# Loading an attention layer's constants through GpSimd's DMA queue instead of SyncE's

## The chip, the core and the metric

The kernel runs on one core of a Trainium2 chip. Such a core has five engines that each work through their own list of instructions in order: TensorE (PE in the profile; its weight loads are listed apart as PEld), VectorE (DVE), ScalarE (ACT), GpSimd (POOL) and SyncE (SP), which here does nothing but issue DMA transfers. Engines wait for one another through semaphores. The metric is the device time of one execution in microseconds (us), as a median over runs; lower is better.

## What is computed

One transformer layer on 256 tokens of width 2048, all in float32: an input projection, three attentions that share it (a forgetting attention with 6 heads, a sparse attention with 4 heads over compressed, selected and windowed keys, and an indexed top-k attention with 6 heads), a gated mixture of the three, and a gated feed-forward layer, each followed by a layer norm; a last gated addition ends it.

```
z = split_cols(h @ w_in[i])
o_fox = fox_attention(q, k, v, z['fox_f'], fox_f_bias[i])
o_nsa = nsa_attention(...)                    # rope, compression with nsa_pe_*, nsa_cmp_*
k_d, v_d = split(rms_norm(z['dsa_ckv'], dsa_kv_norm[i]) @ dsa_kv_up[i], 2)
o_dsa = dsa_attention(apply_rope(...), rope1(k_d, cos, sin), v_d, ...)
mixed = g_fox*(o_fox @ w_br_fox) + g_nsa*(o_nsa @ w_br_nsa) + g_dsa*(o_dsa @ w_br_dsa)
h = layer_norm(ALPHA * h + mixed @ w_out, ln1_g, ln1_b)
a, b = split(h @ w_ffn_in, 2)
h = layer_norm(ALPHA * h + (silu(a) * b) @ w_ffn_out, ln2_g, ln2_b)
h = h + (p @ w_ple_in) * sigmoid(h @ w_ple_gate)
```

Beside the weights the attentions need small constants: an identity matrix, cosine and sine tables for the rotary embedding ("rope"), a triangle of ones, masks, the vectors `dsa_kv_norm` and `fox_f_bias`, and the small matrices `kvup`, `peT` and `cmp2`.

## The kernel before

**Products.** Every float32 factor is split into a rounded part and a remainder (`halves`, line 156): ACT writes the rounded part (`whi`, `k4h`), DVE subtracts it from the source and writes the remainder (`wlo`, `k4l`). A product is then three matmuls: rounded by rounded, rounded by remainder, remainder by rounded (lines 246, 247, 248). The weights of the input projection come in chunks named c1, c2, c3, c4, c6, c5, c7 and f0 to f5. A chunk of 512 columns is loaded in eight groups of 512 KB (`raw<-att_c`, line 170; three `raw` buffers, so that a load waits until DVE has split the group three before it), and each group feeds 12 matmuls of 512 columns. Below, g1 to g8 are the groups of c2, the second chunk, and g9, g10 and so on those of c3.

**Work beside the chunks.** The attentions' own steps are generators that a counter of groups (`tick`) moves on, a few instructions after each group. `after_c1` takes the results of c1: it ropes the index keys (lines 544 to 548), takes a power of the mean square on GpSimd (`rms`, line 632), scales with `gkv` (line 639), transposes on TensorE (line 647), multiplies by `kvup` (line 658), ropes the product into `rc` and transposes it (line 555). A further generator, `prepare`, loads pieces of a later weight (`preb`, `prea`, line 902) and forms differences of them on DVE (lines 904 to 908).

**The constants.** `load` brings in one constant. It first lets GpSimd copy a single element of the newest remainder `wlo` into the destination's corner (line 513), which holds the transfer back until DVE has come that far, and then issues the DMA (line 514). `load_first` loads the first part of the table `cst`, `gkv` and `fbias` and copies the identity out of `cst` on DVE (line 520); `load_rest` loads `kvup`, the second and third part of `cst`, `peT` and `cmp2`. These are eight transfers in all. GpSimd issues no other transfer before the layer norm's parameters (`gb`, line 1090), far behind the attention.

**What sets the order.** The program is written as one stream; when it is built, a scheduler places each engine's instructions by its own estimate of when they can run. An edit of one engine's work can so move instructions on others, and from then on the order on each engine is fixed.

Of the kernel before, what the change touches and what calls it, by code (L numbers as in the profile page):

```python
# [128 lines left out]
def build(ctx: ExitStack, tc: tile.TileContext, A: dict):  # L129
    nc = tc.nc  # L130
# [150 lines left out]
    def pair_gemm(a, b, X, F, seven, kt, pool, banks, mid=None, out=None, slots=None, defer=False, long=0, spare=(),  # L281
# [70 lines left out]

        for p in range(np_ - long):
            ra, rb, raw, x = load(p)
            if p not in seven:
                w = ahead if p == 0 and ahead else [split(ra, "", wp), split(rb, "", wp)]
# [44 lines left out]
        if long:  # L401
            W = []
            for i, p in enumerate(range(np_ - long, np_)):
                ra, rb, _, x = load(p)
                name, q = spare[i - 2] if i >= 2 else ("", wp)
                W.append((p, x, [split(ra, name, q), split(rb, name, q)]))
            for h in range(2):
                for p, x, w in W:
                    plain(p, h, x, w)
                    tick()  # L410
                finals([h])
                if h == 0:
                    between()
            return e
# [48 lines left out]
    with ExitStack() as at:  # L463
# [43 lines left out]
        def load(tile, src, part=None):  # L507

            t = tile if part is None else tile[:, part]
            corner = t  # L510
            while len(corner.shape) > 2:
                corner = corner[:, 0]
            POOL.tensor_copy(corner[:1, :1], newest[0].bitcast(F32)[:1, :1])
            nc.sync.dma_start(t, src if part is None else src[:, part])

        def load_first():
            load(cst, A["consts"], slice(0, n1))
            load(gkv, A["dsa_kv_norm"].partition_broadcast(P))
            load(fbias, A["fox_f_bias"].partition_broadcast(P))
            DVE.tensor_copy(ident, C["ident"])  # L520
            POOL.memset(half_c, -0.5)
# [452 lines left out]
    part = ctx.enter_context(ExitStack())  # L974
# [416 lines left out]
```

## Time and profile before

| What | Value |
| --- | --- |
| Time, median of 3 runs | 1556.35 us (1555.92 to 1556.39) |
| The profiled execution's own time | 1554.99 us |
| Its span, first to last instruction | 1553.2 us |
| TensorE busy | 1544.1 us (99%) |
| DVE busy | 1363.2 us (88%) |
| ACT busy | 879.6 us (57%) |
| POOL busy | 20.8 us (1%), 44 instructions |
| Granted TensorE clock | 1.000 |

Times inside the span are counted from its start. A row of the timeline gives start, duration, engine, line, operation, `out<-in`, how many such instructions, and in brackets how long the engine sat idle before and what ended that. SP's rows (SPq) are the issues of transfers; when a transfer has landed is in the view of DMA issues, as microseconds from issue to landing. In the rows of `order` below, an instruction is given with its line, operation, tiles and shape and no time.

### The profile page before, as it was taken

How to read it: one execution, taken by the hardware profiler on the slowest of the kernel's cores; microseconds unless marked ns; L12 is line 12 of the kernel's file. 1: busy time of each engine (PE TensorE's matmuls, PEld its weight loads, DVE VectorE, ACT ScalarE, POOL GpSimd, SP SyncE). 2: the span in 40 equal slices, each digit the busy share in tenths (PEclk: the TensorE clock that was granted, in tenths of full speed). 3: DMA queues.
4: the chain of work that ended last, by engine and by line, in shares of the span. 5: the costliest groups of instructions: out<-in, count | busy, mean ns of one | idle time of the engine just before them, and what ended most of it. 6: DMA issues, size and time to landing. Idle time of an engine off the chain costs nothing. (4 is left out here: it accounts for less than half of the span.)

```text
span 1553.2 us, 20506 instructions
## 1 busy us (share of the span) xinstructions
PE 1544.1 (99%) x7317; PEld 1288.6 (83%) x7317; DVE 1363.2 (88%) x1909; ACT 879.6 (57%) x1153; POOL 20.8 (1%) x44
## 2 busy tenths in 40 slices
PE   9999999999999999999999999999999999999998
PEld 7778899988888888888788888888888888887887
DVE  6779787569898998998879999999999999989896
ACT  6545566556565555544455656665556666555463
POOL 1000000000000000001000000000000000010000
PEclk9999999999999999999999999999999999999999
DMA  8866888575655574648465667777777776887544
GB/s 293 295 216 215 303 287 290 175 218 207 217 176 186 208 255 155 225 164 298 152 223 188 230 234 246 263 257 264 274 261 268 259 265 227 293 284 250 175 165 135
DMA packets 105575, 360.91 MB, mean 232 GB/s; under 512 B 12033, under 2 KB 13185, under 8 KB 105473
## 3 DMA queue, kind: packets, MB, share of 16 engines
q1 hardware_dynamic: 104192, 355.41, 67.1%
q0 software_dynamic: 1280, 4.20, 0.9%
q8 instruction: 57, 0.93, 0.2%
q14 instruction: 46, 0.37, 0.1%
HBM read 337.54 MB, written 22.02 MB: 231 GB/s over the span
## 5 line engine op out<-in xcount | busy, mean ns | idle before, releaser
L156 ACT ACTIVATE whi<-raw 128x1024 fp32r<-128x1024 f32 (+3 forms) x538 | 507.2, 962 | 338.9 <-PE acc L247 96.3
L156 DVE TENSOR_TENSOR wlo<-raw,whi 128x1024 fp32r<-128x1024 f32 (+3 forms) x538 | 585.5, 1104 | 126.3 <-ACT whi L156 123.5
L246 PE MATMUL acc<-whi,k4h 128*128 128x512 f32 (+3 forms) x724 | 274.9, 380 | 0.5 <-ACT k4h L156 0.3
L247 PE MATMUL acc<-whi,k4l 128*128 128x512 f32 (+3 forms) x724 | 266.9, 369 | 0.8 <-DVE k4l L156 0.8
L248 PE MATMUL acc<-wlo,k4h 128*128 128x512 f32 (+3 forms) x724 | 266.3, 369 | 0.4 <-DVE wlo L156 0.4
L156 ACT ACTIVATE wthi<-raw 128x1024 fp32r<-128x1024 f32 x166 | 175.7, 1060 | 152.8 <-DVE raw L382 92.0
L156 DVE TENSOR_TENSOR wtlo<-raw,wthi 128x1024 fp32r<-128x1024 f32 x166 | 200.0, 1218 | 0.1
L299 PE MATMUL sc<-whi,k4h 128*128 128x512 f32 x488 | 191.2, 392 | 0.0
L300 PE MATMUL sc<-whi,k4l 128*128 128x512 f32 x488 | 190.1, 390 | 0.0
L301 PE MATMUL sc<-wlo,k4h 128*128 128x512 f32 x488 | 189.7, 390 | 0.1
L299 PE MATMUL acc<-whi,k4h 128*128 128x512 f32 x408 | 160.1, 392 | 0.0
L301 PE MATMUL acc<-wlo,k4h 128*128 128x512 f32 x408 | 159.1, 390 | 0.6 <-DVE wlo L156 0.6
L300 PE MATMUL acc<-whi,k4l 128*128 128x512 f32 x408 | 158.9, 389 | 0.0
L246 PEld LDWEIGHTS acc<-whi,k4h 128*128 128x128 f32 x724 | 136.3, 188 | 24.3 <-issue 5.1
L247 PEld LDWEIGHTS acc<-whi,k4l 128*128 128x128 f32 x724 | 136.5, 189 | 18.9 <-DVE k4l L156 1.5
L248 PEld LDWEIGHTS acc<-wlo,k4h 128*128 128x128 f32 x724 | 136.0, 188 | 19.5 <-DVE wlo L156 0.8
L382 DVE TENSOR_TENSOR raw<-raw 128x1024 f32<-128x1024 f32 x78 | 95.1, 1219 | 18.0 <-DMA raw<-ffn_in 6.2
L301 PEld LDWEIGHTS sc<-wlo,k4h 128*128 128x128 f32 x488 | 91.6, 188 | 19.8 <-DVE wlo L156 0.5
L300 PEld LDWEIGHTS sc<-whi,k4l 128*128 128x128 f32 x488 | 91.7, 188 | 18.9
L299 PEld LDWEIGHTS sc<-whi,k4h 128*128 128x128 f32 x488 | 91.6, 188 | 18.7
L301 PEld LDWEIGHTS acc<-wlo,k4h 128*128 128x128 f32 x408 | 76.5, 188 | 17.5 <-DVE wlo L156 1.5
L299 PEld LDWEIGHTS acc<-whi,k4h 128*128 128x128 f32 x408 | 76.7, 188 | 15.4
(381 smaller groups left out, 2115.3 us busy)
## 6 DMA issues: line engine op xcount, KB each, us to landing
raw<-ffn_in SPq DMA_DIRECT2D x169, 512.0 KB, 4.5
raw<-gate SPq DMA_DIRECT2D x96, 512.0 KB, 4.5
raw<-ffn_out SPq DMA_DIRECT2D x88, 512.0 KB, 4.9
raw<-att_c SPq DMA_DIRECT2D x40, 512.0 KB, 4.6
raw<-att_f SPq DMA_DIRECT2D x48, 384.0 KB, 3.9
raw<-ple_gate SPq DMA_DIRECT2D x32, 512.0 KB, 4.4
g<-actd SPq DMA_DIRECT2D x20, 512.0 KB, 4.7
g<-cmp SPq DMA_DIRECT2D x16, 512.0 KB, 5.5
```

Source lines behind the costliest of these rows:

```text
L156: split_last[:] = [ACT.activation(hi, src, AF.Copy).ins, DVE.tensor_sub(lo, src, hi.bitcast(F32)).ins]
L246: PE.matmul(o, xh[:, c], h, start=(k == 0), stop=False)
L247: PE.matmul(o, xl[:, c], h, start=False, stop=False)
L248: PE.matmul(o, xh[:, c], l, start=False, stop=(k == kt - 1))
L299: PE.matmul(o, xh, h, start=first, stop=False)
L300: PE.matmul(o, xl, h, start=False, stop=False)
L301: PE.matmul(o, xh, l, start=False, stop=stop)
L382: DVE.tensor_tensor(t[0], raw[:, 0:1, :].broadcast_to([P, 2, 512]), raw[:, 1:3, :], op=ALU.subtract)
```

## The change

The DMA of `load` is issued by GpSimd instead of SyncE. The same eight transfers, with the same copies in front of them, so leave SP's list and enter GpSimd's.

```diff
             POOL.tensor_copy(corner[:1, :1], newest[0].bitcast(F32)[:1, :1])
-            nc.sync.dma_start(t, src if part is None else src[:, part])
+            nc.gpsimd.dma_start(t, src if part is None else src[:, part])
```

The scheduler then builds three places differently. First the two queues themselves. On GpSimd, around the loads of `load_first` and the start of `load_rest`:

```order
 L513 COPY gkv<-wlo 1x1
 L513 COPY fbias<-wlo 1x1
+L514 DMA cst<-consts 128x448
+L514 DMA gkv<-dsa_kv_norm 128x256
+L514 DMA fbias<-fox_f_bias 128x6
 L513 COPY kvup<-wlo 1x1
+L514 DMA kvup<-kvup 128x512
+L513 COPY cst<-wlo 1x1
+L514 DMA cst<-consts 128x384
 L638 COPY ra<-ra 128x64
-L513 COPY cst<-wlo 1x1
```

The first transfer stands behind three copies, and the copy of `after_c1` (line 638) now stands behind five transfers. On SyncE, from the start of c2's loads:

```order
+L170 DMA raw<-att_c 128x1024 x3
+L902 DMA preb<-ffn_in 128x1024
+L170 DMA raw<-att_c 128x1024 x3
+L902 DMA prea<-ffn_in 128x1024
 L170 DMA raw<-att_c 128x1024
-L514 DMA cst<-consts 128x448
-L514 DMA gkv<-dsa_kv_norm 128x256
-L514 DMA fbias<-fox_f_bias 128x6
```

The loads of g1 to g6 follow one another with only `preb` between them, and `prea` is issued behind g6; before it was issued behind g7.

Second, on DVE, in the middle of c2, where `after_c1` scales its result (line 639):

```order
 L673 SCALAR_TENSOR_TENSOR lf<-lf 128x12
 L904 TENSOR_TENSOR pret<-preb 128x512
+L905 TENSOR_TENSOR pret<-preb,prea 128x512
 L639 SCALAR_TENSOR_TENSOR ra<-acc,rms,gkv 128x256 x2
 L156 TENSOR_TENSOR wlo<-raw,whi 128x1024 x2
```

The instruction that needs `prea` now stands in front of line 639 and of the splits of g5 and g6. On TensorE at the same place:

```order
-L248 MATMUL acc<-wlo,k4h 128x512
 L647 MATMUL sc<-ident,ra 128x128 x4
+L246 MATMUL acc<-whi,k4h 128x512
+L247 MATMUL acc<-whi,k4l 128x512
+L248 MATMUL acc<-wlo,k4h 128x512
```

The first four transposes of what line 639 writes stand six matmuls earlier, directly behind g3's matmuls.

Third, on DVE near the end of c2, in front of the first rope of `rc`:

```order
 L908 TENSOR_TENSOR prea<-prea,preb 128x512
+L156 TENSOR_TENSOR wlo<-raw,whi 128x1024
 L156 TENSOR_TENSOR pret<-pret,prea 128x512
-L156 TENSOR_TENSOR wlo<-raw,whi 128x1024
+L156 TENSOR_TENSOR wlo<-raw,whi 128x1024 x2
 L544 TENSOR_TENSOR rc<-sc,cst 128x128
```

Before, DVE had split eight groups of c2 and c3 ahead of this rope; now ten, so the rope stands behind the splits of g9 and g10.

## The prediction

> **What bounds the kernel now.** I began with the page's busy times and the table by stretches around the change.
>
> ```profile
> PE 1544.1 (99%) x7317; PEld 1288.6 (83%) x7317; DVE 1363.2 (88%) x1909; ACT 879.6 (57%) x1153; POOL 20.8 (1%) x44
> ...
> 0.00:10.00 10.00, 8.21 (x32) 6.62 (x32) 3.17 (x6) 5.15 (x8) 0.34 (x6) 1.00 0.77 251
> ...
> 20.00:30.00 10.00, 10.00 (x47) 8.57 (x46) 6.01 (x13) 5.97 (x14) 2.23 (x5) 1.00 0.75 262
> 30.00:40.00 10.00, 10.00 (x48) 8.30 (x47) 8.22 (x19) 6.39 (x11) 3.07 (x4) 1.00 0.96 337
> 40.00:50.00 10.00, 9.99 (x46) 7.93 (x45) 7.40 (x17) 4.92 (x8) 1.22 (x4) 1.00 0.77 273
> 50.00:60.00 10.00, 9.90 (x50) 8.38 (x51) 9.94 (x21) 5.39 (x9) 0.08 (x1) 1.00 0.91 295
> ```
>
> Columns after the length are the busy time of PE, PEld, DVE, ACT and POOL, then clock, DMA share and GB/s. TensorE sets the time: 9.1 us of the 1553.2 us span are not covered by it, 1.8 of them in the first 10 us, and in the 40 us where the constants are loaded only 0.11. So time can hardly be won here, while any microsecond for which TensorE waits goes into the end: it works in order and has no free time later to make it up.
>
> Next I looked at what SyncE waits for between 18 and 60 us, since that is what the edit takes away.
>
> ```profile
> SPq L514 <- POOL cst L513: 7.1, 2, 4.2
> ...
> SPq L514 <- POOL cmp L513: 5.2, 1, 5.2
> SPq L514 <- POOL gkv L513: 3.4, 1, 3.4
> ...
> SPq L514 <- POOL kvup L513: 1.7, 1, 1.7
> ```
>
> SyncE stands still for 7.1 + 5.2 + 3.4 + 1.7 = 17.4 us behind GpSimd's copies, with weight loads queued behind it. Freeing it lets those loads start earlier, but TensorE has no wait there that they could shorten.
>
> **The change part by part.** *Removed:* the 17.4 us of SyncE's waits, worth at most the 0.11 us above; I take 0. *Kept:* the eight copies and the bytes. *Added:* eight issues on GpSimd. That engine is idle, so the issues cost nothing by themselves; what counts is when the data land and who waits.
>
> *Step 1, the first constants land later.* The instruction that waits is DVE's copy of the identity (line 520), with DVE's split of g1 right behind it.
>
> ```profile
> 21.94 0.58 POOL L513 COPY cst<-wlo 1x1 f32<-1x1 f32 x1 [21.07 <-DVE wlo L156]
> 22.47 0.17 POOL L513 COPY gkv<-wlo 1x1 f32<-1x1 f32 x1
> 22.59 1.17 POOL L513 COPY fbias<-wlo 1x1 f32<-1x1 f32 x1
> ...
> 22.55 0.33 SPq L514 DMA_DIRECT2D cst<-consts  x1
> ...
> cst<-consts SPq DMA_DIRECT2D x1, 224.0 KB, 2.6
> ...
> 25.26 0.23 DVE L520 COPY ident<-cst 128x128 f32<-128x128 f32 x1 [0.94 <-DMA cst<-consts]
> 25.40 1.22 DVE L156 TENSOR_TENSOR wlo<-raw,whi 128x1024 fp32r<-128x1024 f32 x1
> ...
> 29.41 0.39 PE L248 MATMUL acc<-wlo,k4h 128*128 128x512 f32 x1
> ```
>
> Now SyncE issues as soon as the first copy is done, at 22.55, and the table lands 2.6 us later. In the changed list GpSimd issues only behind its third copy, at 22.59 + 1.17 = 23.8. The trace has no constants on GpSimd's queue; the nearest rows are the layer norm's parameters, the first of the bursts at 704, 1362, 1368 and 1378 us:
>
> ```profile
> gb<-ln_g POOLq DMA_DIRECT2D x1, 256.0 KB, 3.8
> ...
> gb<-ln_g POOLq DMA_DIRECT2D x1, 256.0 KB, 6.3
> ...
> gb<-ln_g POOLq DMA_DIRECT2D x1, 256.0 KB, 6.7
> ...
> gb<-ln_g POOLq DMA_DIRECT2D x1, 256.0 KB, 5.8
> ...
> L1090 POOL DMA_DIRECT2D gb<-ln_g x8 | 4.5, 564 | 610.0 <-PE sc L301 605.2 <-PE acc L301 4.8
> ```
>
> 3.8 to 6.7 us from issue to landing bound it: 27.6 to 30.5. I take 5.0, a little above the middle of the lowest two (3.8 and 5.8), since 224 KB is less than 256 but two loads of 512 KB (g3, `preb`) are issued beside it: landing at 28.8. The copy then ends near 28.9 and g1's split, 25.40 less 25.26 behind it and 1.22 long, at 30.3. TensorE needs it at 29.41: it waits **0.9**. At 27.6 the wait is 0; at 30.5 it is 2.6.
>
> The Trainium skill, "DMA: Bandwidth & Descriptors", section "Anatomy of one DMA — SWDGE (gpsimd) path", fits 2.0 us plus bytes over 436 GB/s for a transfer of this queue. That would be some 2.5 us for 224 KB, an estimate from that page; the table would land at 26.3 and this step would cost nothing. The 3.8 to 6.7 us just quoted speak against it in this kernel.
>
> *Step 2, the wait moves to `prea`.* DVE goes on with g2, the first rope and g3; then SyncE may issue g6 and behind it `prea`.
>
> ```profile
> 28.10 0.23 DVE L544 TENSOR_TENSOR ra<-zs,cst 128x64 f32<-128x64 f32 x1 [1.48 <-ACT zs L627]
> ...
> 28.63 0.18 DVE L548 TENSOR_TENSOR ra<-ra,rb 128x32 f32<-128x32 f32 x1
> ...
> 34.62 0.42 SPq L902 DMA_DIRECT2D prea<-ffn_in  x1
> ...
> preb<-ffn_in SPq DMA_DIRECT2D x1, 512.0 KB, 5.0
> ...
> prea<-ffn_in SPq DMA_DIRECT2D x1, 512.0 KB, 6.7
> ...
> 35.00 0.69 DVE L904 TENSOR_TENSOR pret<-preb 128x512 f32<-128x512 f32 x1
> 35.60 0.87 DVE L639 SCALAR_TENSOR_TENSOR ra<-acc,rms,gkv 128x256 f32<-128x256 f32 x2
> ...
> 37.11 0.39 PE L246 MATMUL acc<-whi,k4h 128*128 128x512 f32 x1
> ```
>
> 30.3 + 1.2 (g2) + 0.7 (rope) + 1.2 (g3) = 33.4; with SyncE's 0.4 for g6, `prea` is issued at 33.8, a little before today's 34.62. It landed 6.7 us after its issue, `preb` 5.0; today three loads stand ahead of `prea` within 3 us, in the change two. I take 5.0: 38.8. Line 905 now waits for that, and line 639, which today starts at 35.60, waits behind it: 38.8 + 0.7 (line 905, as line 904) + 0.4 (half of 0.87) = 39.9. The first transposes on TensorE stand where its matmul at 37.11 stood. TensorE is then **2.8 us** behind (the 0.9 of step 1 included, not added). With 27.6 and a landing in 4.6 it would be 1.2; with 30.5 and 6.7, 6.2.
>
> The table lands 3.6 us later than today's 25.2, yet only 2.8 comes through, since DVE's idle gap of 1.48 in front of line 544 takes up the rest.
>
> *Step 3, the rope of `rc` behind g10.*
>
> ```profile
> L156 DVE TENSOR_TENSOR wlo<-raw,whi 128x1024 fp32r<-128x1024 f32 x9 | 10.9, 1214 | 2.7 <-ACT whi L156 2.6
> ...
> 41.47 0.29 DVE L650 COPY nsT<-sc 128x128 f32<-128x128 f32 x1 [1.77 <-ACT nT L649]
> 41.68 0.28 DVE L651 COPY dkT<-sc 128x128 f32<-128x128 f32 x1
> ...
> raw<-att_c SPq DMA_DIRECT2D x1, 512.0 KB, 4.6
> ...
> raw<-att_c SPq DMA_DIRECT2D x1, 512.0 KB, 6.3
> ...
> 49.14 0.28 DVE L544 TENSOR_TENSOR rc<-sc,cst 128x128 f32<-128x128 f32 x1
> ...
> 49.73 0.22 DVE L548 TENSOR_TENSOR rc<-rc,rb 128x64 f32<-128x64 f32 x1
> ...
> 49.94 1.06 ACT L156 ACTIVATE whi<-raw 128x1024 fp32r<-128x1024 f32 x1 [0.67 <-DMA raw<-att_c]
> 50.10 0.30 PE L555 MATMUL sc<-ident,rc 128*128 128x128 f32 x1
> ```
>
> Today the rope ends at 49.95 and TensorE's transpose follows at 50.10 with 0.15 to spare. In the change g10's split stands ahead. Its load needs g7's buffer: 38.8 + 0.7 + 0.9 (line 639) + 3 x 1.2 (g5, g6, g7) + 0.6 (copies) = 44.6. It lands in 4.6 to 6.3 us (g6's row and g10's own); the middle gives 50.0. Then 1.06 on ACT, 1.2 on DVE, 0.8 for the rope: 53.1. TensorE would be **3.0** behind, nearly what step 2 left it with. With 4.6 the step adds nothing to step 2; with 6.3 it makes 3.9.
>
> *Other waits.* `gkv`, `kvup`, the tables' second part and `peT` are needed much later than they land, or in DVE's shadow of steps 1 and 2: cost 0. If `fbias` landed after DVE reached line 669 it would lengthen step 2 by up to 1; that is in the upper bound.
>
> *Sum.* Steps 2 and 3 overlap, so the larger nearly rules: 2.9. On the profiled execution's 1554.99 (span 1553.2 plus 1.8 around it): 1557.9. The median of the runs shown lies 1.36 higher, so the forecast is **1559.3**, 0.19% up. About 0.2%, 3.1 us, is what a measurement of this kernel can tell from no change; the forecast lies just under that line.
>
> **The rivals.** *The cover holds.* GpSimd's first transfer lands as fast as its fastest row or faster, `prea` comes while DVE still works, and TensorE loses 0 to 1.2: 1556.4 to 1557.6, say 1556.9. For it: DVE has idle gaps of 0.9 to 1.8 us there, and SyncE's weight loads come earlier. Against: three of the four first-of-burst rows are at 5.8 or above. (By the Trainium skill's fit, cited in step 1, this case would come about.)
>
> *Late landing, slower beyond doubt.* The first table lands 6.7 us after issue, at 30.5, and pushes every later split: from 29.1 on, step 2 exceeds 3.1 us. With `prea` in 5.0 this makes 30.5 - 28.8 = 1.7 more: 4.5, or 1560.9; with 6.7 too, 1562.6. For it: the transfer shares the DMA engines with two loads of 512 KB, at a DMA share of 0.75 to 0.96. Against: 3.8 in the first burst.
>
> The Trainium skill, "SBUF — State Buffer", section "SBUF: two separate sides", warns that GpSimd cannot write its descriptors while DVE runs a copy in a two-port mode, and tells of some 620 ns that became 3100. As an estimate from that page that is 2.5 us more on the first landing, about 1561.8. The 0.56 us per `gb` issue show no such stretch here, and DVE is idle from 24.3 on (the 0.94 in front of line 520), soon after the first issue.
>
> *SyncE's freedom pays.* Earlier weight loads take away waits beyond 60 us and outweigh steps 1 to 3: at most the 9.1 us not covered by TensorE less the 1.8 in the first 10 us, ahead of the change, or 7.3; with half of that, 1552.7.
>
> *It does nothing.* The two queues could behave alike: 1556.35. The list of GpSimd speaks against that.
>
> **How the numbers follow.** Forecast (1.3 to 4.2 us lost) 0.66; the cover holds 0.15; late landing 0.13; SyncE's freedom 0.04; nothing 0.02. The forecast's own range, 1557.6 to 1560.6, is cut by the line at 1559.46: I give 0.34 below, 0.32 above. Within 0.2%: 0.34 + 0.15 + 0.02 = 0.51. Slower: 0.32 + 0.13 = 0.45. Faster: 0.04. The range takes in half of the cover's case and most of the late one: 1556.8 to 1562.0.
>
> **What would show it.** Step 1: DVE idle in front of line 520 for 3 to 5 us, released by the DMA of `consts`, and a PE wait of up to 2 us at line 248. Step 2: DVE idle in front of line 905, released by `prea`, and a PE wait at line 647. Step 3: L555 behind DVE's rope near 53. SyncE's rows for line 514 are gone. I am wrong if TensorE stays at 10.00 between 28 and 54 us, or if it waits more than 5 us, or if the time moves outside these 30 us.

## The result and the profile after

The changed kernel takes **1564.45 us** in the median (1562.91 to 1569.4 in 6 runs), the kernel before, run beside it, 1556.77 us (1555.92 to 1560.02). The ratio is 1.0051, with a 95% interval of 1.0037 to 1.0064: the change costs 0.51%, 5.8 to 10 us. The profiled execution takes 1564.3 us with a span of 1562.5, against 1553.2 before.

Most of the lost time lies where it was looked for. The first matmul of the indexer's scores, behind the ropes and transposes that the first constants feed, starts at 66.58 us before and at 73.07 after, as the timelines of the two kernels show (columns: start, length, engine, line, operation).

```profile
66.58 0.50 PE L740 MATMUL sc<-dkT,iq 64*128 64x128 f32 x4
```

```profile
73.07 0.50 PE L740 MATMUL sc<-dkT,iq 64*128 64x128 f32 x4
```

That is 6.5 us; the text below calls it the *delay at the scores*. The waits of TensorE (24 to 62 us) and of VectorE (20 to 62 us) after the change; before it the view lists none of TensorE's there:

```profile
PE sc L647 <- DVE ra L639: 2.8, 1, 2.8
PE acc L248 <- DVE wlo L156: 1.7, 1, 1.7
...
DVE ident L520 <- DMA cst<-consts: 5.8, 1, 5.8
...
DVE pret L905 <- DMA prea<-ffn_in: 2.2, 1, 2.2
```

Both waits that the prediction named are there. Step by step, in the timeline after:

```profile
23.59 0.70 POOL L514 DMA_DIRECT2D cst<-consts  x1
...
29.97 0.23 DVE L520 COPY ident<-cst 128x128 f32<-128x128 f32 x1 [5.76 <-DMA cst<-consts]
...
31.36 3.22 SPq L170 DMA_DIRECT2D raw<-att_c  x3
31.39 0.50 PE L248 MATMUL acc<-wlo,k4h 128*128 128x512 f32 x1 [1.66 <-DVE wlo L156]
...
34.63 0.42 SPq L902 DMA_DIRECT2D prea<-ffn_in  x1
...
41.06 0.69 DVE L905 TENSOR_TENSOR pret<-preb,prea 128x512 f32<-128x512 f32 x1 [2.21 <-DMA prea<-ffn_in]
41.67 0.87 DVE L639 SCALAR_TENSOR_TENSOR ra<-acc,rms,gkv 128x256 f32<-128x256 f32 x2
...
42.20 0.66 PE L647 MATMUL sc<-ident,ra 128*128 128x128 f32 x4 [2.81 <-DVE ra L639]
```

The table lands some 6.3 us after its issue (23.59 to the copy's 29.97, less a little), `prea` 6.4 us after its own (34.63 to 41.06). The view of DMA issues for 22 to 36 us has both (columns: count, size, median us to landing):

```profile
preb<-ffn_in SPq DMA_DIRECT2D x1, 512.0 KB, 8.1
prea<-ffn_in SPq DMA_DIRECT2D x1, 512.0 KB, 6.4
...
cst<-consts POOLq DMA_DIRECT2D x1, 224.0 KB, 6.3
```

One thing was not foreseen at all. Right behind the wait at line 647 the table by stretches shows a clock under 1.00 (sixth number behind the length):

```profile
43.00:44.00 1.00, 1.00 (x5) 0.82 (x4) 1.00 (x2) 1.00 (x2) 0.26 (x1) 0.72 0.38 152
44.00:45.00 1.00, 1.00 (x3) 0.76 (x3) 1.00 (x3) 0.14 (x1) 0.85 (x1) 0.50 0.69 82
45.00:46.00 1.00, 1.00 (x4) 0.75 (x3) 1.00 (x3) 0.00 (x0) 0.61 (x1) 0.50 0.65 221
46.00:47.00 1.00, 1.00 (x4) 0.75 (x3) 0.34 (x1) 0.00 (x0) 0.00 (x0) 0.57 0.91 352
```

TensorE counts as busy in all four rows and does only 3 to 5 matmuls in each. The lost clock is 0.28 + 0.50 + 0.50 + 0.43 = 1.7 us.

### The profile page after: what moved, and what is told of

Same layout as the page of the kernel before. It is cut to its first block, busy times and chain, and to the rows that moved or that the text cites. A ratio compares the mean times of both kernels' runs of the same rounds, so it can differ in the third digit from the quotient of the medians.

```text
span 1562.5 us, 20510 instructions
## 1 busy us (share of the span) xinstructions
PE 1546.9 (99%) x7317; PEld 1289.7 (83%) x7317; DVE 1363.0 (87%) x1909; ACT 879.3 (56%) x1153; POOL 26.9 (2%) x52
## 5 line engine op out<-in xcount | busy, mean ns | idle before, releaser
L246 PEld LDWEIGHTS acc<-whi,k4h 128*128 128x128 f32 x724 | 136.6, 189 | 24.8 <-issue 4.9
L247 PEld LDWEIGHTS acc<-whi,k4l 128*128 128x128 f32 x724 | 136.9, 189 | 18.8 <-DVE k4l L156 1.3
L300 PEld LDWEIGHTS acc<-whi,k4l 128*128 128x128 f32 x408 | 76.7, 188 | 15.5
```

The costliest lines, as they stand in the source:

```text
L246: PE.matmul(o, xh[:, c], h, start=(k == 0), stop=False)
L247: PE.matmul(o, xl[:, c], h, start=False, stop=False)
L300: PE.matmul(o, xl, h, start=False, stop=False)
```

## The experiments

For the first four runs there were three theories. A: three costs add up, the late first table (2.0 us), the wait of line 905 for `prea` ahead of line 639 (3.1) and the half clock (1.7). B: whatever goes through GpSimd's queue slows the loads that SyncE issues beside it, whatever the order. C: the new order alone, line 905 ahead of 639, makes the cost.

The timed runs of one kernel scatter by some 3 us on either side, so one profile can be off by as much. The times below are medians of several runs, with the ratio to the kernel before, run beside them, and its 95% interval.

### Only the first table back on SyncE

```diff
-            load(cst, A["consts"], slice(0, n1))
+            load(cst, A["consts"], slice(0, n1), nc.sync)
```

> Only the first table (cst, first part) goes back to SyncE's queue; the other seven constants stay on GpSimd's. Line 905 still stands ahead of line 639. Theory A (three terms: the first table's late landing 2.0 us, line 905's wait for prea ahead of line 639 3.1 us, and a half clock behind that wait 1.7 us): the wait at line 248 is gone, prea is issued 1 to 2 us earlier, TensorE waits at line 647 for 1 to 2 us, the clock stays full: 1 to 2.5 us above the kernel before. Theory B (whatever is on GpSimd's queue slows SyncE's weight loads): seven of eight transfers remain, about 6 above. Theory C (the new order alone, line 905 ahead of line 639): about 5 above, with the half clock.

Measured: 1562.51 us against 1557.16, ratio 1.0035 (1.0018 to 1.0052). The table lands in 2.6 us, and the cost stays. From the waits of TensorE and the view of DMA issues in this run:

```profile
PE sc L647 <- DVE ra L639: 3.5, 1, 3.5
```

```profile
raw<-att_c SPq DMA_DIRECT2D x5, 512.0 KB, 7.6
preb<-ffn_in SPq DMA_DIRECT2D x1, 512.0 KB, 9.2
...
cst<-consts SPq DMA_DIRECT2D x1, 224.0 KB, 2.6
```

So the late table isn't the main cost, and A's sum falls. B and C are both left: line 905 is still ahead of 639 and waits 2.6 us for `prea`, and SyncE's loads are among the slowest of all the runs.

### Only the first table on GpSimd

```diff
-            nc.sync.dma_start(t, src if part is None else src[:, part])
+            (q or nc.sync).dma_start(t, src if part is None else src[:, part])
...
-            load(cst, A["consts"], slice(0, n1))
+            load(cst, A["consts"], slice(0, n1), nc.gpsimd)
```

> The kernel before with only the first table (cst, first part) on GpSimd's queue; the other seven constants on SyncE's. Line 639 stands ahead of line 905. Theory A: DVE waits 4 to 6 us at line 520, TensorE about 2 us at line 248 and up to 1 at line 647, full clock: 2 to 3.5 above before. Theory B: one of eight transfers, below 1 above. Theory C: 0.

Measured: 1560.06, ratio 1.0016 (1.0006 to 1.0026). Line 639 is ahead of 905 here, and TensorE has no wait at lines 248 and 647, but one of 1.8 us at 555, for the rope of `rc` behind an extra split: the prediction's step 3 in the open. The 2.9 us lie in A's range, but neither of the waits that A named is there, and C's 0 is missed.

### The difference loads begin four groups later

```diff
-... (9, 2, "heads"), (10, 2, "heads"))), 26
+... (9, 2, "heads"), (10, 2, "heads"))), 30
```

> The changed kernel with prepare's first job starting four groups later, so that lines 904 and 905 no longer stand ahead of line 639; all eight constants on GpSimd's queue. Theory A: the 2.0 us at line 248 stay, at most 1.5 more at line 647, no half clock: 2 to 4 above before. Theory B: about 7.7 above, as the change. Theory C: 0 to 1 above.

Measured: 1563.18, ratio 1.0030 (1.0020 to 1.0041). In its profile the half clock near 43 us and the wait at line 647 are gone and the delay at the scores is 2.3 us, but the edit moves all loads of `prepare`, and a later wait of 2.3 us, ahead of 832 us and with a half clock behind it, is new. The profile is that of the slowest of its ten runs. This run decides nothing.

### The wait at line 647 filled with matmuls

Twelve matmuls on data at hand, whose result nobody reads, stand ahead of the first transposes, so that TensorE doesn't idle:

```diff
+                for _ in range(12 if h == 0 else 0):
+                    PE.matmul(tp, X(0)[0][:, :P], newest[0], start=True, stop=True)
                 for i in range(4):
                     PE.transpose(tp[:, i * P:(i + 1) * P], ts[h][:, i * P:(i + 1) * P], ident)
```

> The changed kernel with 12 matmuls whose result nobody reads (2.7 us at 0.227 each) directly ahead of the first transposes of line 647, so that TensorE is busy while DVE waits for prea. Theory A: the waits stay, the clock stays full: 1.7 us below the changed kernel, about 6 above before. If the half clock costs nothing that isn't hidden: as the changed kernel, or up to 0.5 above it.

Measured: 1564.62, ratio 1.0043 (1.0031 to 1.0055), no better than the change itself. The clock stays at 1.00: with TensorE kept busy, no half clock follows. But the waits of TensorE move on (line 649 is 647 here):

```profile
PE sc L555 <- DVE rc L548: 1.5, 1, 1.5
PE sc L649 <- DVE ra L639: 0.5, 1, 0.5
```

The half clock's 1.7 us are real in the profile and not seen in the time: when they are saved, TensorE comes to line 555 earlier and waits there. (VectorE's order moved a little with the edit, so that the half clock costs nothing in the end is likely, and not shown.)

The four runs gave the theories another form. S: the delays add up. M: they stand in a row, TensorE is late by what the last of them makes it, and with that gone the next one decides. T: GpSimd's transfers hold back SyncE's loads.

### The changed kernel again

> The changed kernel once more, as the base for the three runs beside it. All theories: 6.5 to 8.5 us above the kernel before. What is open is the half clock: if 2.8 us without a matmul at the transposes of L647 is what halves it, the profile shows a granted clock of 0.5 for one window right behind that wait whenever the wait begins early in a window, and full clock otherwise.

Measured: 1563.26 against 1557.92, ratio 1.0034 (1.0021 to 1.0046). That is 5.3 us above the kernel before, less than the 6.5 to 8.5 expected and than the 7.7 of the first runs: the cost of the change itself is known to some 2 us only. In this profile the table lands 5.0 us after issue and TensorE does not wait at line 248, but all the longer at 647; the half clock follows again. Waits of TensorE and VectorE, and two stretches:

```profile
PE sc L647 <- DVE ra L639: 4.0, 1, 4.0
...
DVE pret L905 <- DMA prea<-ffn_in: 2.9, 1, 2.9
DVE ident L520 <- DMA cst<-consts: 2.3, 1, 2.3
```

```profile
42.00:43.00 1.00, 1.00 (x5) 0.89 (x4) 1.00 (x2) 1.00 (x3) 0.15 (x1) 0.50 0.43 172
43.00:44.00 1.00, 1.00 (x4) 0.72 (x3) 1.00 (x2) 0.26 (x2) 0.96 (x1) 0.50 0.45 61
```

1.7 + 2.8 = 4.5 us of waits in one execution and 4.0 in the other: what isn't lost at the first place is lost at the second.

### The copy of the identity behind the first rope

```diff
-            DVE.tensor_copy(ident, C["ident"])
...
-                rope(zs[:, h, :64], ..., t[:, 384:448])
+                with tc.issue_after(rope(zs[:, h, :64], ..., t[:, 384:448])): DVE.tensor_copy(ident, C["ident"]) if not h else 0
```

> The changed kernel with the copy of the identity (L520), which is the first reader of the first table, moved on VectorE behind the splits of g1 and g2 and the first rope; nothing else moves. Theory S (the delays add up): the 2.0 us that TensorE loses at L248 goes, so 5.5 to 6 us above the kernel before instead of 7.7. Theory M (the delays are in a row and the last one decides): TensorE gets to L647 2 us sooner and waits 2 us longer there for VectorE, which waits for prea at L905, so nothing is won: 7 to 8.5 us above. Theory T (GpSimd's transfers hold SyncE's back): as M, with g2 and g3 still landing 7 us after issue.

Measured: 1564.61, ratio 1.0043 (1.0031 to 1.0056). The 6.7 us above the kernel before lie between S's range and M's, and against the change beside it nothing is won, as M says. VectorE no longer stands still for the table ahead of g1's split, and TensorE still waits at line 647, with the half clock behind it:

```profile
PE sc L647 <- DVE ra L639: 3.0, 1, 3.0
```

```profile
DVE pret L905 <- DMA prea<-ffn_in: 0.7, 1, 0.7
```

Line 905 waits only 0.7 us for `prea` here. VectorE also waits 1.9 and 1.2 us for the rounded halves of g3 and g4, and lines 904 and 905 are themselves 1.2 us of work ahead of line 639. The delay at the scores in this one execution is 4.1 us, less than in either profile of the change (70.64 us against 73.07 and 71.88), which the times of the six runs don't show.

### Lines 904 and 905 behind line 639

```diff
+                with tc.issue_after(first[0]) if ... else nullcontext():
-                DVE.tensor_sub(t[:, 0, :], rb[:, 0, :], rb[:, 1, :])
-                DVE.tensor_sub(t[:, 1, :], rb[:, 0, :], ra[:, 0, :])
+                    DVE.tensor_sub(t[:, 0, :], rb[:, 0, :], rb[:, 1, :])
+                    DVE.tensor_sub(t[:, 1, :], rb[:, 0, :], ra[:, 0, :])
```

> The changed kernel with the first pair of L904 and L905 put behind L639 on VectorE by an edge of order, so that nothing ahead of TensorE's transposes waits for prea. Theory S: 3.1 us of the wait and 1.7 us of the half clock go, 2.0 us of the first landing and perhaps 1 us at L555 stay: 2 to 4 us above the kernel before. Theory M: the same, 2 to 4 us, since with the last wait gone the one ahead of it decides. Theory T: g2, g3 and preb still land 7 to 8 us after issue and the splits behind them stay late, so at most 1 us is won: 6.5 to 7.5 us above.

Measured: 1560.26, ratio 1.0015 (1.0005 to 1.0025), 3.0 us less than the change beside it. The wait at 647 and the half clock are gone; the clock is 1.00 in every stretch. What is left is step 3, one wait of TensorE:

```profile
PE sc L555 <- DVE rc L548: 1.8, 1, 1.8
```

VectorE still waits 2.5 us for the table at line 520, and TensorE isn't reached by it. `prea` still lands 6.0 us after issue. This is the run that carries the explanation: the same transfers and the same place of the transposes on TensorE, another place for two instructions of VectorE (what hangs on them, down to the splits of `preb` and `prea`, moved back with them). The intervals of the two ratios, 1.0005 to 1.0025 here and 1.0021 to 1.0046 for the change, hardly overlap. M and S both said 2 to 4 us; T's 6.5 to 7.5 is missed.

### Only gkv and fbias on GpSimd

```diff
-            load(gkv, A["dsa_kv_norm"].partition_broadcast(P))
-            load(fbias, A["fox_f_bias"].partition_broadcast(P))
+            load(gkv, A["dsa_kv_norm"].partition_broadcast(P), q=nc.gpsimd)
+            load(fbias, A["fox_f_bias"].partition_broadcast(P), q=nc.gpsimd)
```

> The kernel before with only gkv and fbias, the two loads that are copied to all partitions from one row, moved to GpSimd's queue; the first table stays on SyncE. Theories S and M: no table is late and L905 stays behind L639, so 0 to 1 us above the kernel before, within what can be told from nothing. Theory T: the loads that SyncE issues in the same microseconds land 7 to 8 us after issue instead of 4, as in the run with only the first table on SyncE, so 3 to 6 us above.

Measured: 1560.52, ratio 1.0015 (1.0006 to 1.0023). The 2.6 us are more than S and M said and less than T's 3 to 6. SyncE's loads land late, as T says. From the view of DMA issues (22 to 35 us) and the waits of ScalarE, which before the change waits 10.7 us for `raw`:

```profile
raw<-att_c SPq DMA_DIRECT2D x4, 512.0 KB, 7.8
preb<-ffn_in SPq DMA_DIRECT2D x1, 512.0 KB, 8.8
```

```profile
ACT whi L156 <- DMA raw<-att_c: 16.2, 10, 5.9
```

How much of that reaches the time isn't settled by this profile: TensorE waits only 0.5 us at line 248 and 0.5 at 647, and a half clock from 11.8 to 15.2 us, ahead of the constants, takes 1.7 us of its own.

### One split moved behind the first rope of rc, with the order of line 905 mended

```diff
-                with behind():
+                with behind(), tc.issue_after(roped[2]) if len(roped) > 2 and since_rope(roped) == 2 else nullcontext():
                     hi, lo = weight_group(...)
```

> The changed kernel with L904 and L905 behind L639, as in the run before, and with one weight split moved behind the first rope of rc, so that four splits stand ahead of that rope as in the kernel before, not five. Theory M (the last wait ahead of TensorE decides, and with it gone the next one): the 2.0 us wait at L555 goes and the run comes to 0 to 1 us above the kernel before. Theory T (GpSimd's transfers hold SyncE's loads back, whatever the order): the splits stay late for their data, 2 to 3 us above, as without this edit.

Measured: 1561.73 against 1557.57, ratio 1.0030 (1.0018 to 1.0042); M's 0 to 1 us is missed, and T's 2 to 3 as well. In this execution the table landed late again (6.3 us), and with no wait at 647 to cover it the wait at line 248 (249 here) counts in full:

```profile
PE acc L249 <- DVE wlo L156: 2.1, 1, 2.1
PE sc L556 <- DVE rc L549: 1.8, 2, 1.3
```

So S isn't wholly wrong: a delay counts as long as no later one swallows it.

### The constants split between the queues, in three ways

The loads of `load_first` stay on SyncE and only those of `load_rest` go to GpSimd (`gkv` and `fbias` are edited as `cst`; the diff is against the changed kernel):

```diff
-            nc.gpsimd.dma_start(t, src if part is None else src[:, part])
+            (q or nc.gpsimd).dma_start(t, src if part is None else src[:, part])
...
-            load(cst, A["consts"], slice(0, n1))
+            load(cst, A["consts"], slice(0, n1), nc.sync)
...
```

> The kernel before with only load_rest (kvup, the second and third part of the tables, peT, cmp) on GpSimd's queue; cst's first part, gkv and fbias on SyncE. L905 is behind L639. Theories M and T: no table is waited for early, no copied row shares the queue with g2 to prea, so 0 to 1 us above the kernel before; T would allow 1 to 2 for kvup and the second part, which meet g4 to g6. A third theory, that any load on GpSimd costs by itself: 3 to 4 us, in proportion to five loads of eight.

Only `load_first` goes to GpSimd (the same with the two queues exchanged):

> The kernel before with only load_first (cst's first part, gkv, fbias) on GpSimd's queue, and load_rest on SyncE. The transfers of the first microseconds are then those of the changed kernel, but L905 stands behind L639, as before the change. Theory M: the cost of the order is gone, 1 to 3.5 us above the kernel before, with no wait over 1.5 us at L647 and full clock there. Theory T: the whole cost comes from these transfers, 5 to 8 us above.

The change, with `gkv` and `fbias` back on SyncE:

> The changed kernel with gkv and fbias back on SyncE; cst's first part and load_rest stay on GpSimd's queue. With this L905 comes behind the first split pair of L639 on VectorE, as it does in the kernel before. Theory M: 1 to 3 us above the kernel before, as with the first table alone on GpSimd's queue. Theory T: 1 to 3 us too, but by another way: g2 and preb land 4 to 5 us after issue instead of 6 to 8.

```diff
-            load(gkv, A["dsa_kv_norm"].partition_broadcast(P))
+            load(gkv, A["dsa_kv_norm"].partition_broadcast(P), q=nc.sync)
```

Measured, in the same order: 1560.89, 1562.38 and 1563.39; ratios 1.0029 (1.0016 to 1.0041), 1.0037 (1.0025 to 1.0050), 1.0035 (1.0023 to 1.0047). All three have line 639 ahead of 905, full clock near 40 us, and no wait of TensorE over 1.7 us, yet each costs 3 to 6 us, more than M said. The third theory of the first run, a cost of any load on GpSimd's queue, said 3 to 4 us there and met the 3.3 measured; T came near in the second (4.8 us; it said 5 to 8). The waits, for the first and the third:

```profile
PE sc L555 <- DVE rc L548: 2.3, 2, 1.7
PE sc L555 <- DVE ra L548: 1.1, 1, 1.1
```

```profile
PE sc L555 <- DVE rc L548: 1.4, 1, 1.4
PE sc L647 <- DVE ra L639: 0.8, 1, 0.8
```

The first has none of the early constants on GpSimd and loses 3.4 us at line 555, where splits and ropes share VectorE. For the third the waits cover 2.2 us of the 2.9 by which the profiled execution (1560.45 us) lies above the kernel before; that the median of its 5 runs lies 5.8 above stays unexplained.

### All three places of the order mended

> The changed kernel with all three places of VectorE's order mended together: the copy of the identity behind the first rope, L904 and L905 behind L639, and four splits ahead of the first rope of rc. All constants still go through GpSimd's queue. Theory M (the waits of VectorE's order are the whole cost, the last of them deciding): 0 to 1.5 us above the kernel before, no wait of TensorE over 1 us between 25 and 60 us. Theory T (GpSimd's transfers slow the loads that SyncE issues beside them): 2.5 to 4 us above, as the runs with one or two orders mended, with TensorE waiting for splits whose raw data land 6 to 8 us after issue.

All constants stay on GpSimd. The edges put in, together:

```diff
+                with tc.issue_after(roped[0]): DVE.tensor_copy(ident, C["ident"]) if not h else 0
...
+                with tc.issue_after(first[0]) if ... else nullcontext():
...
+                with behind(), tc.issue_after(roped[2]) if len(roped) > 2 and since_rope(roped) == 2 else nullcontext():
```

Measured: 1559.83 against 1557.89, ratio 1.0020 (1.0009 to 1.0031). Between M (0 to 1.5 us) and T (2.5 to 4). TensorE's waits between 24 and 62 us:

```profile
PE sc L556 <- DVE rc L549: 1.8, 2, 1.0
PE sc L649 <- DVE ra L641: 0.2, 1, 0.2
```

Three mended places take the 5.3 to 7.7 us of the change down to 1.9 (3.1 by the ratio): so 2 to 6 us of the change are VectorE's order (the interval lies below that of the change's first runs and overlaps that of its second). What remains shows at the ropes of `rc`, and the trace finds more of the order there. VectorE's second split of `preb`, which waits for ScalarE, which had waited 2.8 us for the transfer that takes `preb` away, stands ahead of the second rope here:

```profile
54.47 0.69 DVE L156 TENSOR_TENSOR preb<-preb 128x512 fp32r<-128x512 f32 x1 [1.25 <-ACT preb L156]
55.08 0.28 DVE L545 TENSOR_TENSOR rc<-sc,cst 128x128 f32<-128x128 f32 x1
...
56.03 0.30 PE L556 MATMUL sc<-ident,rc 128*128 128x128 f32 x1 [1.01 <-DVE rc L549]
```

In the kernel before it comes 9 us behind that rope (and in the change it is behind, too):

```profile
52.18 0.28 DVE L544 TENSOR_TENSOR rc<-sc,cst 128x128 f32<-128x128 f32 x1
...
61.75 0.69 DVE L156 TENSOR_TENSOR preb<-preb 128x512 fp32r<-128x512 f32 x1 [1.26 <-ACT preb L156]
```

So a fourth place of the order differs here. The same split stands ahead of that rope in the run with one split moved (TensorE waits 1.3 us there) and in the one with only `load_rest` on GpSimd (1.7). All eight loads stay on GpSimd's queue in this run, and it costs about what one, two or five of them cost (ratio 1.0020 against 1.0016, 1.0015 and 1.0029), so a cost in proportion to the loads isn't borne out. But every run that takes constants off SyncE's queue also differs from the kernel before in VectorE's order, so what the transfers alone cost isn't shown, and the costs of the runs that move only some of the loads don't add up to the whole.

### The kernel before again

> The kernel before once more, for a second profile of it: 0 us, within 1 us of the runs beside it. What is open: in the profiles the stretch from the first matmul of the indexer's scores (dkT, iq) to the last matmul lasts 1482.6 us before and 1482.5 to 1485.6 us in the runs with constants on GpSimd's queue. If that spread is scatter between executions, this profile shows 1483 to 1486; if those runs lose time there too, it shows 1482 to 1483 again.

Measured: 1557.25, ratio 1.0000 (0.9990 to 1.0011). Its profile gives two things. The scores start at 66.91 us, and from there to the last matmul it takes 1484.8 us, against 1482.5 in the first profile of this same kernel. The other profiles have 1482.5 to 1486.2 (1492.3 in that of the later loads), so most of that spread is scatter between executions. And the loads of `prepare` are slow here as well:

```profile
preb<-ffn_in SPq DMA_DIRECT2D x1, 512.0 KB, 6.4
prea<-ffn_in SPq DMA_DIRECT2D x1, 512.0 KB, 6.5
...
cst<-consts SPq DMA_DIRECT2D x1, 224.0 KB, 2.5
```

### The constants on ScalarE's queue

```diff
-            nc.gpsimd.dma_start(t, src if part is None else src[:, part])
+            nc.scalar.dma_start(t, src if part is None else src[:, part])
```

> The changed kernel with its constants issued by ScalarE's queue instead of GpSimd's, so that SyncE is as free as in the changed kernel and no transfer goes through GpSimd's queue; the order follows (preb and prea two and five places earlier on SyncE, L905 still ahead of L639). Theory M: prea is issued some 8 us sooner and lands ahead of L905's turn, but TensorE still waits for whatever VectorE has late: -1 to 3 us. Theory T: the loads land 4 to 5 us after issue again, -1 to 1 us. The rival that SyncE's freedom pays: 1 to 2 us faster than the kernel before.

Measured: 1563.32, ratio 1.0040 (1.0028 to 1.0052). All three theories miss. SyncE is as free as in the change, nothing passes GpSimd's queue, and the table is late all the same, with `preb` and `prea` going out beside it; VectorE's copy of the identity, ahead of one more pair of splits in this order, holds the low half of X that TensorE needs. The view of DMA issues (21 to 32 us) and the waits of TensorE:

```profile
preb<-ffn_in SPq DMA_DIRECT2D x1, 512.0 KB, 6.6
prea<-ffn_in SPq DMA_DIRECT2D x1, 512.0 KB, 7.9
cst<-consts ACTq DMA_DIRECT2D x1, 224.0 KB, 6.6
```

```profile
PE acc L247 <- DVE k4l L156: 3.4, 1, 3.4
```

No run came out faster than the kernel before; a version that beats both was not found.

## Why the prediction was wrong

The direction held; the size was out by 5 us (1559.3 forecast, 1564.45 measured, above the range).

**Step 1, the mechanism right, the landing a little short.** The issue at 23.8 and VectorE's wait at line 520 came as described (23.59; 5.8 us). The landing was taken at 5.0 us; it took 4.5 to 6.3 in the profiles with all the constants on GpSimd, 6.3 in the change's first and 5.0 in its second. TensorE lost 1.7 us at line 248 where 0.9 was said, or none. (The 28.9 at which the prediction has the copy end is its start; the 30.3 that it goes on with is right.) With the copy moved away (the identity's run) no time was won.

**Step 2 is the step that failed, by its size.** The wait at line 905, behind it 639, behind that TensorE at 647: all there. The term that was mis-sized is the landing of `prea`. The prediction quoted its row, 6.7 us, and took 5.0, `preb`'s, because two loads instead of three would stand ahead of it. Three still do (SP's row at 31.36), and it took 6.4 and 6.5 in the two profiles of the change, 6.7 and 6.5 in those of the kernel before. It was also issued 0.8 us later than the 33.8 said, behind the later table. With both, 34.6 + 6.4 + 1.1 = 42.1 for the end of line 639's first half, as measured, in place of 39.9. TensorE comes out 5.1 us late at line 647 (42.20 against the 37.11 of the matmul whose place it takes), not 2.8.

**What was missing: the half clock.** 2.8 us without a matmul were followed by 3.4 us at half clock, 1.7 us more. No step looked at what a wait of TensorE does to its own clock; the sum put it at nothing. With the clock the delay at the scores is 6.5 us (5.0 in the second profile of the change, measured against the second of the kernel before). That is 3.6 us above the 2.9 of the sum; the medians missed by 4.8 in the first runs (7.7 less 2.9) and by 2.4 in the second (5.3 less 2.9).

**Step 3** is real (1.8 us at line 555 in two runs) and was covered, as "overlaps" said, by a step 2 larger than it.

**The sum.** Taking the largest instead of adding was right for the change, as the identity's run shows; with the wait at line 647 gone, the others count each for itself, as in the run with one split moved. **SyncE's freedom** paid nothing in any run, also not with ScalarE's queue. **The late landing** as a rival described the first profile of the change closely: the table after 6.3 us (it said 6.7), `prea` after 6.4 (6.7) and TensorE 5.1 late (4.5 to 6.2). Its 1560.9 to 1562.6 still fell short, for want of the half clock, and the second profile, with the table in 5.0, shows that the wait at line 647 comes without so late a table. The Trainium skill's warning of stretched descriptor writing ("SBUF — State Buffer", "SBUF: two separate sides") didn't show: the issues took 0.53 to 0.70 us each, and one of the copies ahead of them, 1.18 long, is as it was before (1.17). VectorE stood idle from 24.2 us to the copy at 29.97, so the first landing put that warning to little test. The Trainium skill's fit of 2.0 us plus bytes over 436 GB/s ("DMA: Bandwidth & Descriptors", "Anatomy of one DMA — SWDGE (gpsimd) path") would give 2.5 us as an estimate; 3.9 to 6.3 were measured with other loads in flight.

## What to carry to other kernels

An engine that waits before it issues also holds back the loads behind. In the kernel before, SyncE issues nothing between the load at 18.88 us and the table at 22.55; the small table landed in 2.5 to 4.1 us in the five profiles with it on SyncE's queue. On another engine's queue it went out among SyncE's 512 KB loads and took 3.9 to 6.6. That these loads are the reason is likely, and not shown by a run of its own. When a scheduler lays out the order, look at which instructions of the waiting engines changed places, since a good part of the cost (3.0 us of 5.3 in one pair of runs) went with two instructions put back, and price a load by its own row, not by a faster neighbour's. Where several waits stand in a row ahead of one engine, the last one can cover the others, and mending one shows the next: a gain must be tried with all of them mended, and each mending can move something else.

## What the runs showed of the hardware

The clock dropped behind windows that were far from empty. In the profiles it changes on a grid of 3.41 us: each half clock inside the run lasts 3.41, and the full clock ahead of it 37.55 us after the change and 34.13 in its second profile, eleven and ten times that. Cut along that grid, TensorE's busy time after the change, as the profile counts it, is (first number behind the length):

```profile
29.79:33.20 3.41, 1.81 (x8) 1.51 (x9) 3.23 (x10) 1.84 (x6) 1.51 (x2) 1.00 0.35 85
...
40.02:43.43 3.41, 1.23 (x8) 1.10 (x9) 2.37 (x4) 2.19 (x4) 0.00 (x0) 1.00 0.97 396
```

Behind the first window, 53% busy, the clock stayed; behind the second, 36%, came 3.41 us at half. In the other profiles windows of 4, 5, 31, 39 and 41% were followed by half clock and those of 46 and 49% not; one of 53%, at 8 us in the run with only `gkv` and `fbias` on GpSimd, was, against the rest, so a share alone doesn't settle it. The Trainium skill, "TensorE: Matmul & The Clock Gate", section "What's actually happening", puts the drop behind at least one idle window of about 3.4 us. The length of the window agrees; that it has to be idle does not: windows 31 to 41% busy were enough.

Another queue is no second path. The table on ScalarE's queue took 6.6 us, as long as the slowest on GpSimd's. The Trainium skill says as much in "DMA: Bandwidth & Descriptors", section "Issuing engines are not separate DMA queues": all issuing engines' transfers run on the same 16 DMA engines and interleave. This run agrees, as far as one latency can.

With `gkv` and `fbias`, which are copied from one row to all partitions, on GpSimd's queue and the first table on SyncE's, SyncE's 512 KB loads landed after 7.6 and 7.8 us (median, 22 to 35 us) in two profiles, against 4.6 and 4.9 in the kernel before. Where the first table was on GpSimd's queue too, nine profiles have 5.1 to 6.7 (the change itself 5.5 twice). So the two alone don't set it, and why the loads slow isn't shown.
